# Weight loads moved to GpSimd's queue, three raw weight buffers for two, and v reordered from SyncE's queue

## The chip, the cores and the metric

The kernel runs on one core of one Trainium2 chip. The metric is the device time of one execution in microseconds (us). Before the change it is 1954.86 us, the median of three runs (1954.16 to 1957.37).

The engines are named TensorE (PE in the profile, PEld for its weight loads), VectorE (DVE), ScalarE (ACT), GpSimd (POOL) and SyncE (SP). SP computes nothing; it issues transfers, in the order of its program.

## The reference, cut to what matters

Two layers of a decoder trunk on 512 tokens of width 1024, in float32:

```python
for l in range(DEPTH):                                  # 2
    h = rms_norm(x, ln1_g[l])
    z = h @ w_in[l]
    xr, gr, q, k, v, g_rnn, g_att = jnp.split(z, cuts, axis=-1)
    xr = causal_depthwise_conv(xr, rnn_conv_w[l], rnn_conv_b[l])
    hr = rg_lru(xr, lru_wa[l], lru_ba[l], lru_wx[l], lru_bx[l], lru_lambda[l])
    y_rnn = hr * jax.nn.gelu(gr)
    y_att = dilated_attention_mixer(q, k, v, positions, q_norm_g[l], k_norm_g[l])
    merged = sigmoid(g_rnn) * (y_rnn @ proj_rnn[l]) + sigmoid(g_att) * (y_att @ proj_attn[l])
    x = x + merged @ w_out[l]
    h2 = rms_norm(x, ln2_g[l])
    u = causal_depthwise_conv(h2 @ w_up[l], ffn_conv_w[l], ffn_conv_b[l])
    u_gate, u_val = jnp.split(u, 2, axis=-1)
    x = x + (jax.nn.gelu(u_gate) * u_val) @ w_down[l]
```

The attention has three groups of four heads with dilations 1, 4 and 16; q and k are normalized and rotated. Groups with a dilation above 1 regroup the tokens into streams (t = m * dilation + r), so q, k and v have to be put into that order of tokens.

## The kernel before, in words

Every product of weights is made of three float32r matmuls: both operands are split into a high part and a low part, and high x high, high x low and low x high are summed. So a weight unit (256 rows x 512 columns, 512 KB) is loaded into a raw buffer `wraw`, ScalarE casts it to `whi` (line 229), VectorE subtracts to make `wlo` (line 234), and TensorE runs 24 matmuls with it (lines 259 to 261). There are some 320 units, in one fixed order, four (sometimes two or six) to a group of 512 output columns; `whi` and `wlo` have three buffers, `wraw` has RAW = 2.

In the loop over units, `prefetch_hi` casts the unit two ahead at the start of a unit, and `prefetch_lo`, in its middle, makes `wlo` of that unit and then calls `load(u + RAW)`. `load` (line 406) issues on SP. A buffer of `wraw` can be overwritten when `wlo` of the unit that lay in it is done, so SP's program holds a wait for VectorE ahead of each load.

A planner writes the order of the rest while the program is built. Work beside the matmuls is cut into chains; each step of a chain says which engine it needs, at what planned time (T["pe"], T["dve"], T["act"]) and how many buffers (20-odd `slot`s of 128x512, 12 `quad`s of 128x2048). Between matmuls `offer` takes the first chain whose step fits; a step for "pe" fits once TensorE's planned time is 1.5 us (MARGIN) past its due time. Engines then run their programs in order.

A step that the attention needs often is `turn` (line 376): VectorE transposes 32x32 blocks into a slot (line 382), SP issues four writes of 64 KB to HBM (line 388) and, one later step on, one read back (line 391); ScalarE copies the returned block (line 229) into a `quad`. There are 80 turns, 40 in each layer. SP also moves the statistics of the softmax (lines 781, 801, 802), the norm gains (line 613) and x.

v comes from groups v0, va and vb. `V.end` (line 705) marks a group done. For va and vb GpSimd's queue writes the four evicted blocks to HBM (line 711), waits until they have landed, and reads them back in the other order of tokens (line 712); `v_done[...].end` is the time at which the planner takes them for usable. `HOP` is 6500 ns.

Of the kernel before, what the change touches and what calls it, by code (L numbers as in the profile page):

```python
# [15 lines left out]
F32 = mybir.dt.float32  # L16
# [7 lines left out]
L, S, D, FF, NH = 2, 512, 1024, 3072, 12  # L24
EPS = 1e-6
BIG = 1e30
NQ = 12
NS = 21
LOOK = 2
RAW = 2  # L30
BACK = 1500.0
BACK_END = 600.0
MARGIN = 1500.0
HOP = 6500.0
# [23 lines left out]
IN_ORDER = ("N1", "N2", "v0")  # L58
# [118 lines left out]
def need(eng, t=0.0, at=0, s=0, q=0, y=0, after=()):  # L177

    return {"eng": eng, "t": t, "at": at, "s": s, "q": q, "y": y, "after": after}


def trunk(tc, wst, lruw, xT, pos, par, gqk, cst, yT):
    from contextlib import ExitStack
    nc = tc.nc
    with ExitStack() as ctx:
# [3 lines left out]
        dr = ctx.enter_context(tc.tile_pool(name="dr", bufs=4, space=bass.MemoryType.DRAM))  # L189
# [5 lines left out]
        for i in range(NQ):  # L195
            cp.tile([128, 4, 512], F32, name="quad", tag=f"quad{i}", bufs=1)
        for i in range(NS):
            cp.tile([128, 512], F32, name="slot", tag=f"slot{i}", bufs=1)
# [6 lines left out]
        T = {"pe": 0.0, "dve": 0.0, "act": 0.0, "table": ""}  # L205
# [22 lines left out]
        def copy(out, src, dep=0.0):  # L228
            nc.scalar.copy(out, src)  # L229
            T["act"] = max(T["act"], dep) + 93.0 + 0.834 * size(out)  # L230
            return T["act"]

        def tt(out, a, b, op, dep=0.0):
            nc.vector.tensor_tensor(out, a, b, op=op)  # L234
            return on_dve(size(out), dep)
# [19 lines left out]
        def rr(ap):  # L255
            return ap.bitcast(F32R)
# [29 lines left out]
        def start(gen, prio=None):  # L286
            if prio is None:
                serial[0] += 1
                prio = serial[0]
            c = Chain(gen, prio)  # L290
            c.step()
            if not c.done:
                chains.append(c)
                chains.sort(key=lambda c: c.prio)
            return c
# [48 lines left out]

        quads, sslots, place = list(range(NQ)), list(range(NS)), {}

# [52 lines left out]
        raws, halves, units = {}, {}, {}  # L399

        def load(upto):
            while unit_no[0] <= upto and unit_no[0] < NUNITS:
                u = unit_no[0]
                raws[u] = ring.tile([128, 1024], F32, name="wraw", tag="wraw", bufs=RAW)
                if u:
                    nc.sync.dma_start(raws[u], wst[u])
                else:
                    for k, queue in enumerate((nc.scalar, nc.sync)):
                        load_x(xT, nc.sync, k + 1)
                        queue.dma_start(raws[0][:, k * 512:k * 512 + 512], wst[0, :, k * 512:k * 512 + 512])  # L410
                unit_no[0] += 1

        def prefetch_hi(upto):
            while unit_no[1] <= upto and unit_no[1] < NUNITS:
                u = unit_no[1]
                load(u)
                raw = raws.pop(u)
                hi = whis[u % 3]
                halves[u] = (raw, hi, copy(rr(hi), raw, T["pe"] if u > LOOK else 0.0))
                unit_no[1] += 1  # L420

        def prefetch_lo():
            for u in list(halves):
                raw, hi, t = halves.pop(u)
                lo = wlos[u % 3]
                units[u] = (hi, lo, tt(rr(lo), raw, hi, ALU.subtract, t))
                load(u + RAW)

        x, xquad, at_x = [None] * 8, [], [0]

        def load_x(src, queue, upto=8):

            while len(xquad) < 2:
                q = qalloc()
                for i in range(4):
                    x[4 * len(xquad) + i] = q[:, i]
                xquad.append(q)
                at_x[0] = 0
            while at_x[0] < upto:
                c = at_x[0]  # L440
                queue.dma_start(x[c], src[c * 128:c * 128 + 128, :])
                at_x[0] += 1
# [14 lines left out]
        for i in range(9):  # L457
            nc.tensor.matmul(spin, idle[:, 0:128], idle, start=True, stop=True)
        nc.scalar.dma_start(prm[0][:, 0:P_CW], par[0, :, 0:P_CW])
        load(0)  # L460
        load(1)
        load_x(xT, nc.sync, 4)
# [141 lines left out]
        qkt, vt, yatt, rope_chain, att_chain, v_done = {}, {}, {}, {}, {}, {}  # L604

        class QK:
# [16 lines left out]
            def end(self):  # L623
                c = rope_chain[self.name] = start(self.chain())
                self.prio = c.prio
# [71 lines left out]
        class V:  # L697
# [6 lines left out]

            def end(self):
                vt[self.name] = self.t
                v_done[self.name].done = True
                v_done[self.name].end = T["act"]
                if self.name not in IN_ORDER:
                    d = dr.tile([S, 512], F32, name="vorder", tag="vorder", bufs=2)  # L710
                    nc.gpsimd.dma_start(d.rearrange("(b p) c -> p b c", p=128), self.t)
                    nc.gpsimd.dma_start(self.t, d.rearrange("(p r) c -> p r c", r=4))
                    v_done[self.name].end += 2 * HOP

        def score_steps(half, s, p0, st0):

# [444 lines left out]
        for k in range(2):  # L1161
            ks = slice(k * 512, k * 512 + 512)
            push(operand[k])
            t = copy(rr(hi[:, ks]), raw[:, ks])
            push(operand[k])
            t = tt(rr(lo[:, ks]), raw[:, ks], hi[:, ks], ALU.subtract, t)
# [13 lines left out]
        u = 0  # L1180
        for l, name, _, nk, k0, _ in GROUPS:
# [13 lines left out]
            for uu in range(nk // 2):  # L1195
# [38 lines left out]
                hi, lo, t = units.pop(u)  # L1234
# [62 lines left out]
```

## Time and profile before

| | us |
|---|---|
| median of three runs | 1954.86 |
| the profiled execution | 1954.35 |
| its span (first to last instruction) | 1952.6 |
| TensorE busy | 1868.8 |
| VectorE busy | 1306.6 |
| ScalarE busy | 967.2 |
| GpSimd busy | 5.6 |

The mean granted clock of TensorE is 0.978. The table is an average over stages that differ: the q, k, v projections with the attention (about 50 to 350 us, and 1020 to 1345 us in the second layer), the recurrent branch and the output projection, and the feed-forward part. The profile is read by stage, and an engine's idle time is followed back through the engine that it waited for, until a transfer or an engine that was busy ends the search.

### The profile page before, as it was taken

To read this page: it belongs to the slowest core of one execution; us is meant where nothing else is said; L and a number is where in the kernel's file an instruction comes from. 1 tells how busy PE (TensorE), PEld (TensorE's weight loads), DVE (VectorE), ACT (ScalarE), POOL (GpSimd) and SP (SyncE) were. 2 spreads that over 40 slices of the span, in tenths; PEclk is the share of its full clock that TensorE was granted. 3 is DMA by queue.
4 is the path that set the end of the run, shared out by engine and by line. 5 is a ranking of instruction groups with operands and counts; after the bars stand their busy time and mean duration, and the time that the engine had idled before them with its cause. 6 is when DMAs were issued, how large, how long until landed. Compare 5 with 4: busy or idle time off the path is not lost.

```text
span 1952.6 us, 22350 instructions
## 1 busy us (share of the span) xinstructions
PE 1868.8 (96%) x8249; PEld 1535.6 (79%) x8249; DVE 1306.6 (67%) x1938; ACT 967.2 (50%) x1655; POOL 5.6 (0%) x12
## 2 busy tenths in 40 slices
PE   9999888999899999999998998989989999999999
PEld 7777776887688888888887786778867888888887
DVE  7768886677656773577476697865875567635762
ACT  7567744577234442344364786455772444313431
POOL 0000000000000000000000000000000000000000
PEclk9999998999899999999999998989999999999999
DMA  4666655432322222222336566455223222322222
GB/s 170 161 172 171 174 137 133 128 111 83 111 95 97 98 97 97 98 97 95 121 121 167 169 162 172 135 137 152 83 76 120 96 98 98 107 98 87 97 104 91
DMA packets 244494, 235.01 MB, mean 120 GB/s; under 512 B 183456, under 2 KB 184736, under 8 KB 243872
## 3 DMA queue, kind: packets, MB, share of 16 engines
q1 hardware_dynamic: 238208, 224.89, 37.5%
q0 software_dynamic: 1664, 8.39, 1.2%
q8 instruction: 65, 1.06, 0.2%
q10 hardware_dynamic: 4512, 0.30, 0.2%
q14 instruction: 45, 0.37, 0.1%
HBM read 204.64 MB, written 28.88 MB: 120 GB/s over the span
## 4 chain that ended last, share of the span: by engine, by line
PE 69%; DVE 12%; DMA 8%; ACT 5%; SPq 4%; issue 2%; ACTq 0%; DVEq 0%
PE acc L259 22%; PE acc L260 22%; PE acc L261 22%; DVE slot L234 5%; DMA slot<-turn 3%; SPq L388 3%; DVE wlo L234 3%; DVE quad L234 2%; DMA turn<-slot 2%; ACT junk L223 1%; ACT whi L229 1%; ACT quad L229 1%; ACT quad L223 1%; DMA stats<-st 1%; DVE slot L382 1%
## 5 line engine op out<-in xcount | busy, mean ns | idle before, releaser
L229 ACT CAST whi<-wraw 128x1024 fp32r<-128x1024 f32 (+1 forms) x321 | 334.7, 1043 | 544.6 <-PE acc L260 482.6
L234 DVE TENSOR_TENSOR wlo<-wraw,whi 128x1024 fp32r<-128x1024 f32 (+1 forms) x321 | 390.0, 1215 | 206.7 <-ACT whi L229 206.6
L259 PE MATMUL acc<-xh,whi 128*128 128x512 f32 x1280 | 506.0, 395 | 13.7 <-ACT quad L223 10.8
L260 PE MATMUL acc<-xl,whi 128*128 128x512 f32 x1280 | 503.3, 393 | 0.0
L261 PE MATMUL acc<-xh,wlo 128*128 128x512 f32 x1280 | 503.1, 393 | 0.0
L259 PEld LDWEIGHTS acc<-xh,whi 128*128 128x128 f32 x1280 | 243.6, 190 | 65.8 <-ACT quad L223 12.9
L261 PEld LDWEIGHTS acc<-xh,wlo 128*128 128x128 f32 x1280 | 243.3, 190 | 51.6
L260 PEld LDWEIGHTS acc<-xl,whi 128*128 128x128 f32 x1280 | 243.6, 190 | 49.6
L259 PE MATMUL acc<-quad,whi 128*128 128x512 f32 x640 | 252.0, 394 | 22.1 <-ACT quad L229 22.0
L260 PE MATMUL acc<-quad,whi 128*128 128x512 f32 x640 | 251.8, 393 | 0.9 <-DVE quad L234 0.9
L261 PE MATMUL acc<-quad,wlo 128*128 128x512 f32 x640 | 250.6, 392 | 0.0
L259 PE MATMUL acc<-whi,xh 128*128 128x512 f32 x576 | 229.3, 398 | 11.6 <-ACT quad L223 6.0
L260 PE MATMUL acc<-wlo,xh 128*128 128x512 f32 x576 | 227.5, 395 | 4.8 <-DVE wlo L234 4.8
L261 PE MATMUL acc<-whi,xl 128*128 128x512 f32 x576 | 227.2, 394 | 0.0
L259 PEld LDWEIGHTS acc<-quad,whi 128*128 128x128 f32 x640 | 121.2, 189 | 51.0 <-ACT quad L229 26.1
L234 DVE TENSOR_TENSOR slot<-acc,rbc 128x512 f32<-128x512 f32 x112 | 77.1, 689 | 109.9 <-PE acc L261 109.9
L260 PEld LDWEIGHTS acc<-quad,whi 128*128 128x128 f32 x640 | 121.1, 189 | 28.9 <-DVE quad L234 3.9
L261 PEld LDWEIGHTS acc<-quad,wlo 128*128 128x128 f32 x640 | 121.2, 189 | 24.9
L259 PEld LDWEIGHTS acc<-whi,xh 128*128 128x128 f32 x576 | 109.8, 191 | 37.0 <-ACT quad L223 7.3
L260 PEld LDWEIGHTS acc<-wlo,xh 128*128 128x128 f32 x576 | 109.7, 190 | 28.5 <-DVE wlo L234 6.8
L229 ACT CAST quad<-slot 128x256 fp32r<-128x256 f32 (+1 forms) x104 | 62.3, 638 | 138.9 <-DMA slot<-turn 127.9
L261 PEld LDWEIGHTS acc<-whi,xl 128*128 128x128 f32 x576 | 109.5, 190 | 23.4
(136 smaller groups left out, 1940.9 us busy)
## 6 DMA issues: line engine op xcount, KB each, us to landing
wraw<-wst SPq DMA_DIRECT2D x319, 512.0 KB, 3.2
turn<-slot SPq DMA_DIRECT2D x288, 64.0 KB, 3.0
slot<-turn SPq DMA_DIRECT2D x48, 256.0 KB, 3.9
quad<-turn SPq DMA_DIRECT2D x24, 256.0 KB, 4.1
quad<-xT SPq DMA_DIRECT2D x16, 256.0 KB, 6.0
vorder<-quad POOLq DMA_DIRECT2D x4, 1024.0 KB, 7.1
quad<-vorder POOLq DMA_DIRECT2D x4, 1024.0 KB, 5.5
slot<-gqk SPq DMA_DIRECT2D x12, 256.0 KB, 3.6
```

The costliest lines, as they stand in the source:

```text
L223: nc.scalar.activation(out, src, func, **kw)
L229: nc.scalar.copy(out, src)
L234: nc.vector.tensor_tensor(out, a, b, op=op)
L259: nc.tensor.matmul(ps, rr(ah), rr(bh), start=first, stop=False)
L260: nc.tensor.matmul(ps, rr(ah), rr(bl), start=False, stop=False)
L261: nc.tensor.matmul(ps, rr(al), rr(bh), start=False, stop=last)
L382: nc.vector.transpose(w, t)
L388: nc.sync.dma_start(v[:, :, i], w[32 * i:32 * i + 32].rearrange("c (j e r) -> c j e r", j=n, e=4))
```

## The change

Four things in the diff. RAW becomes 3 and NS, the number of slots, 20. `load` issues unit 4 and later ones on GpSimd's queue, units 1 to 3 as before on SP. The reordering of va and vb becomes a chain of its own, `reorder`, with the highest priority: one step issues the write on SP once TensorE's planned time is 1.5 us past the planned eviction, another issues the read on SP 8 us of planned time later, and v counts as usable HOP after that. For v0 nothing is reordered, as before. The change's summary in words also names "a returning block expected one us later"; no line of the diff does that, and line 392 keeps its 4000.

```diff
-NS = 21
+NS = 20
 LOOK = 2
-RAW = 2
+RAW = 3
@@ load
                 if u:
-                    nc.sync.dma_start(raws[u], wst[u])
+                    (nc.sync if u < 4 else nc.gpsimd).dma_start(raws[u], wst[u])
                 else:
@@ class V
             def end(self):
                 vt[self.name] = self.t
+                if self.name not in IN_ORDER:
+                    start(self.reorder(T["act"]), 1)
+                else:
+                    v_done[self.name].done = True
+                    v_done[self.name].end = T["act"]
+
+            def reorder(self, t):
+                yield need("pe", t)
+                d = dr.tile([S, 512], F32, name="vorder", tag="vorder", bufs=2)
+                nc.sync.dma_start(d.rearrange("(b p) c -> p b c", p=128), self.t)
+                yield need("pe", T["pe"] + HOP)
+                nc.sync.dma_start(self.t, d.rearrange("(p r) c -> p r c", r=4))
                 v_done[self.name].done = True
-                v_done[self.name].end = T["act"]
-                if self.name not in IN_ORDER:
-                    d = dr.tile([S, 512], F32, name="vorder", tag="vorder", bufs=2)
-                    nc.gpsimd.dma_start(d.rearrange("(b p) c -> p b c", p=128), self.t)
-                    nc.gpsimd.dma_start(self.t, d.rearrange("(p r) c -> p r c", r=4))
-                    v_done[self.name].end += 2 * HOP
+                v_done[self.name].end = T["pe"] + HOP
```

## Rows read from the trace of the kernel before

**Rows 1.** Busy time by stretch (us); then TensorE's granted clock, DMA share, GB/s.

```profile
50.00:350.00 300.00, 271.35 (x1219) 222.75 (x1218) 229.10 (x408) 179.92 (x429) 2.75 (x4) 0.95 0.58 155
...
79.10:82.40 3.30, 3.30 (x10) 2.53 (x9) 1.80 (x4) 1.98 (x5) 0.00 (x0) 0.50 0.59 215
...
500.00:1020.00 520.00, 517.55 (x2281) 427.19 (x2280) 317.73 (x403) 204.58 (x270) 0.00 (x0) 1.00 0.30 104
1020.00:1345.00 325.00, 300.07 (x1338) 246.32 (x1337) 235.54 (x416) 196.18 (x445) 2.61 (x4) 0.95 0.58 158
```

**Rows 2.** Waits, whole span: waiter <- awaited: us in total, times, longest.

```profile
ACT quad L229 <- DMA slot<-turn: 127.9, 30, 10.0
```

**Rows 3.** SP's own waits, first in 50 to 350 us, then in 1020 to 1345.

```profile
SPq L406 <- DVE wlo L234: 64.8, 19, 8.6
...
SPq L406 <- DVE wlo L234: 82.9, 26, 10.1
```

**Rows 4.** Timeline, 52 to 80 us: start, us, engine, line; brackets: idle before, releaser.

```profile
55.13 1.89 DVE L382 STREAM_TRANSPOSE slot<-slot 128x512 f32<-128x512 f32 x3
...
52.02 9.35 SPq L406 DMA_DIRECT2D wraw<-wst  x2
61.41 8.18 SPq L388 DMA_DIRECT2D turn<-slot  x12
...
74.74 1.93 ACT L229 CAST quad<-slot 128x512 fp32r<-128x512 f32 x3 [7.89 <-DMA slot<-turn]
...
78.64 0.50 PE L259 MATMUL acc<-whi,xh 128*128 128x512 f32 x1 [3.42 <-ACT quad L223]
```

**Rows 5.** Timeline, 261 to 282 us.

```profile
261.05 0.71 DVE L382 STREAM_TRANSPOSE slot<-slot 128x512 f32<-128x512 f32 x1
...
266.38 0.33 SPq L406 DMA_DIRECT2D wraw<-wst  x1
266.76 3.11 SPq L388 DMA_DIRECT2D turn<-slot  x4
...
275.07 1.23 ACT L229 CAST quad<-slot 128x256 fp32r<-128x256 f32 x2 [9.51 <-DMA slot<-turn]
...
281.83 0.36 PE L754 MATMUL at<-quad 128*128 128x256 f32 x1 [2.96 <-DVE quad L234]
```

**Rows 6.** Timeline, 1195 to 1226 us.

```profile
1195.91 7.07 SPq L388 DMA_DIRECT2D turn<-slot  x10
...
1205.13 8.75 SPq L388 DMA_DIRECT2D turn<-slot  x12
...
1209.33 1.19 ACT L229 CAST quad<-slot 128x256 fp32r<-128x256 f32 x2 [4.83 <-DMA slot<-turn]
...
1222.23 1.19 ACT L229 CAST quad<-slot 128x256 fp32r<-128x256 f32 x2 [7.81 <-DMA slot<-turn]
...
1224.81 0.55 PE L851 MATMUL y<-quad 128*128 128x256 f32 x1 [4.55 <-DVE quad L234]
```

**Rows 7.** Issues and landings of writes (L388), loads (L406), v (L711, L712); ns min/median/max.

```profile
L388 SPq DMA_DIRECT2D turn<-slot x320: 569/627/2752, 61.4 to 1336.4; - x160
...
DMA to landing us min/median/max: 2.0/2.8/7.4
...
L406 SPq DMA_DIRECT2D wraw<-wst x319: 327/328/2384, 2.1 to 1923.5; - x160
...
wraw<-wst SPq DMA_DIRECT2D x319, 512.0 KB, 3.2
...
quad<-vorder POOLq DMA_DIRECT2D x4, 1024.0 KB, 5.5
...
L711 POOL DMA_DIRECT2D vorder<-quad x4: 757/757/891, 105.2 to 1213.8; - x4
L712 POOL DMA_DIRECT2D quad<-vorder x4: 547/548/549, 112.2 to 1222.5; - x4
...
DMA to landing us min/median/max: 5.0/6.6/8.2
```

## The prediction, made before the changed kernel was run

> **What bounds the kernel now.** I read the stretches first, then the waits, and last the timelines of SP's queue beside ScalarE and TensorE. From 500 to 1020 us TensorE is busy 517.55 of 520 us at full clock: 2281 matmuls, 0.227 us each, so a weight unit of 24 matmuls is 5.45 us, and nothing that only moves data makes this stretch shorter [rows 1]. The two attention stretches are different: 28.7 us idle of 300 and 24.9 us idle of 325, 53.6 us together, at a granted clock of 0.95. A mean of 0.95 between two levels of 1.0 and 0.5 is a tenth of the time at the lower one, 30 + 32.5 = 62.5 us, and one such short stretch is among the rows. At 90% busy, half speed loses 62.5 x 0.9 x 0.5 = 28 us. The attention stretches could thus give back at most 53.6 + 28 = 82 us. One long stall in each layer lies outside them, in the recurrent branch between ScalarE and VectorE; the change does not touch it.
>
> What makes TensorE idle there: ScalarE waits 127.9 us, 30 times, for a returned `slot<-turn` block [rows 2], and it is in order, so evictions and weight casts stand behind that wait. I followed the 19 idle times of TensorE over 0.8 us in the two stretches (50.7 us, first at 75, last at 1292) back the same way; 16 of them go to a late turn. Why late: SP issues the turn's four writes and its read, and also every weight load, and a load's line first waits until VectorE has finished `wlo` of the unit that held the buffer. In that one wait SP stands 64.8 of the 300 us and 82.9 of the 325 us [rows 3].
>
> Three cases. First: three transposes are done by 57.0 us, SP stands in line 406 from 52.0 to 61.4, the first write leaves at 61.4, ScalarE waits 7.89 us, TensorE 3.42 us [rows 4]. Second: transposed by 261.8, next a load that leaves at 266.4, writes at 266.8, ScalarE waits 9.51, TensorE 2.96 [rows 5]. Third, the other kind: between 1195.9 and 1213.9 SP issues 22 writes nearly back to back; a read behind them comes late, ScalarE waits 7.81, TensorE 4.55 [rows 6]. A write takes SP 0.63 us, a load 0.33 [rows 7].
>
> **The change part by part.** *Loads leave SP's queue.* From unit 4 on, line 406 issues on GpSimd's queue, which otherwise holds nothing any more. Behind a load's wait there now stand only later loads. For each of the 19 idle times I took from SP's timeline the time that SP spent in line 406 (waiting and issuing) between the transpose and its first write, and between the landing of the writes and the read; the saving is the smaller of this and the idle time. Example: rows 4 give 61.4 - 57.0 = 4.4 for the last of the three transposes and a microsecond more for the first, so all 3.42 go; rows 5 give 4.95, so all 2.96 go; rows 6 give only a load's issue on the write's way and one on the read's, 1.3 of 4.55. Summed so: 16.6 us in layer 0 and 13.1 us in layer 1, 29.7 of 50.7. Six of the 19 follow another within 14 us, and the turns behind them are already in flight when the earlier one is shortened; they carry 8.7 us, which I count at nothing. Left: 21 us. The lower clock comes behind such stalls (the stretch at 0.50 begins half a microsecond after the stall of 3.42 us ends, [rows 1, 4]), so I give back the same share, 28 x 21/53.6 = 11 us. What is late next is SP's own issue, four times 0.63 us for a turn, which stays.
>
> *Faster landing of turns.* Writes land in 2.0 us at best and 2.8 in the median [rows 7]. They no longer stand in one queue behind a 512 KB load, but the load still uses the same DMA engines. Bounds: 0.8 us for a write and as much for a read in each of the 19, 0 to 30 us, capped by the idle that is left; I take 0 and keep 15 for the range.
>
> *Does a load on GpSimd's queue come in time?* The trace has no load there. The nearest rows are the eight transfers of v, 1 MB each: issue 0.55 to 0.89 us, landing 5.0 to 8.2 us; the load itself lands from SP in 3.2 us in the median [rows 7]. So 3.5 to 9.1 us altogether; I take 4.5, nearer the row of the same size. With three raw buffers a load waits for the cast three units back, not two, and is needed 2.5 units later, not 1.5: 13.6 us against 8.2. Even 9.1 is covered: cost nothing, and the cover is gone above 13.6 us. ScalarE's waits for weights should nearly vanish, but they hardly ever end an idle time of TensorE, so I take nothing for them.
>
> *v goes through SP in two steps.* Two issues for each of four groups, about 0.76 + 0.55 us on SP [rows 7]. The write's step waits for ScalarE's last eviction of v, the read's step for the landing; behind either stand turns and the small transfers of the statistics. The write's wait: 0, or as long as ScalarE stood before such an eviction, 4.83 us [rows 6]; the code puts the step 1.5 us behind the planned eviction, so I take 1. The read's step comes 8 us after the write by the plan, and a landing takes up to 8.2 us [rows 7], so 0.2. Two of the four (the last, at 1213.8 us, and its twin in layer 0) fall into crowded stretches of SP: 2 x (1.31 + 1.2) = 5 us. Bounds 0 to 4 x (1.31 + 4.83) = 25 us. The users of v come a group later, so its planned end, some 3 us later, costs nothing.
>
> *20 slots for 21.* A gain is excluded, unless by a chance shift of order; a chain that finds no slot goes later. Bounds -5 to 10 us (one more wait as long as ScalarE's longest, [rows 2]); I take 0. *The first three loads* stay on SP, and the second of them no longer waits: 0, within 1 us either way.
>
> The sum: -21 - 11 + 5 = -27 us. The profiled execution took 1954.35 (span 1952.6 and 1.75 around it), 0.5 under the median of the three runs, so 1954.9 - 27 = 1928 us.
>
> **The rivals.** *All of it comes:* the six close stalls too (29.7, and 28 x 29.7/53.6 = 15 of clock), the landing 15, v free: 1954.9 - 60 = 1895. For it: SP's longest waits all go. Against: the third case. 0.13.
>
> *Little:* the load's line is only where SP happens to stand, and the turn waits as long elsewhere. Then only issue time is saved, two loads of 0.33 us in each of 13 stalls, 8.6 us, with 4 of clock, less 5 for v: 1947. For it: the third case, and 0.63 us for every write. Against: in one stretch SP waits 64.8 us in that line [rows 3], and its issues are 0.33. 0.12. The Trainium skill (DMA: Bandwidth & Descriptors, § Issuing engines are not separate DMA queues) says that issuing from several engines saves only the sequencer's issue time; by that rule this rival holds and the time is 1947. Rows 3 and 4 speak against the rule here, as what holds SP is a wait ahead of the issue.
>
> *Slower:* GpSimd's queue takes one load at a time. It decides from 5.45 us a load on, the time of a unit. If a load there took as long as v's read, 0.55 + 5.5 = 6.05 us [rows 7], then the 95 loads of 500 to 1020 us [rows 1] cost 0.6 us each, 57 us, and as much in the second layer: 1928 + 114 = 2042. For it: in the trace no two transfers of that queue are in flight together. Against: half the bytes, and 3.2 us from SP. 0.06. The Trainium skill (SBUF — State Buffer, § SBUF: two separate sides) says that VectorE can keep GpSimd from writing descriptors while an operation holds the port that they share; by that rule a load would come later by up to one operation of VectorE, and this rival would be likelier. Rows 7 show GpSimd's issues at 0.55 to 0.89 us in stretches where VectorE was busy three quarters of the time [rows 1], so no hold of that kind is seen.
>
> *The order shifts* with one slot less and v's later plan, and new stalls of the present size appear, eight of 3 us, 24, with 13 of their clock, beyond what is saved by 7: 1962. For it: the order is made by a greedy list. Against: nothing of the plan's engine times changes. 0.08. *The change doesn't do what it says:* its summary names a later return, which the diff lacks; I go by the diff, and no chance is kept for it.
>
> **How the numbers follow.** Forecast 1928 with 0.61, its own range 1911 to 1948 (landing 15, v's bound 20 more). All of it 0.13, little 0.12, slower 0.06 and 0.08. The range leaves out the first of the slower ones, half of the second, and part of the lower rival: 1900 to 1960. A measurement here can tell about 0.2% from no change, 3.9 us. Faster: 0.61 + 0.13 and a third of little, as 1947 with v at its bound is no gain, 0.78; same 0.07; slower 0.15.
>
> **What would show it.** Right: SP has no waits in line 406 in the attention stretches; the writes leave within 1 us of the transpose in the first two cases; ScalarE's wait for `slot<-turn` falls from 127.9 to about 80 us; TensorE's idle in the two stretches falls from 53.6 to about 37 us, the clock there rises from 0.95 to 0.97; the stretch from 500 to 1020 stays. Wrong: loads on GpSimd's queue land above 13 us, or ScalarE waits longer for weights; SP waits long in v's two steps; the writes leave late behind other lines.

## The result and the profile after

The changed kernel takes 1923.41 us, the median of four runs (1921.61 to 1927.58), beside 1956.11 us for the kernel before on the same chip (1954.16 to 1957.80). The ratio is 0.9836, 95% interval 0.9815 to 0.9857: 32 us faster, 28 to 36. The profiled execution of the changed kernel is the longest of its four, 1927.58 us with a span of 1925.6, against 1954.35 and 1952.6 before. Of all executions behind this document one, of the kernel raw3_late below, took 3107.92 us at a mean granted clock of 0.555, and is left out of its numbers.

First the sum. The page's line of busy times and the two shares of the chain that ended last, changed kernel:

```profile
PE 1859.5 (97%) x8249; PEld 1532.2 (80%) x8249; DVE 1306.7 (68%) x1938; ACT 969.2 (50%) x1655; POOL 167.9 (9%) x320
...
PE 79%; DVE 7%; ACT 5%; DMA 5%; SPq 2%; issue 2%; ACTq 0%; DVEq 0%
```

TensorE runs the same matmuls. Its busy time fell from 1868.8 to 1859.5 us (9.3), its idle time, span less busy, from 83.8 to 66.1 (17.7); together 27.0, the whole difference of the spans. So there is nothing to look for but two things: shorter stalls, and matmuls that run at a higher clock.

Second, where. Busy time by stretch, changed kernel; columns as in [rows 1]. The second attention stretch lies 20 us earlier here:

```profile
50.00:350.00 300.00, 281.08 (x1281) 232.81 (x1280) 238.26 (x424) 189.82 (x444) 23.86 (x45) 0.96 0.62 162
500.00:1000.00 500.00, 500.00 (x2209) 413.75 (x2208) 305.48 (x384) 197.24 (x256) 48.26 (x91) 1.00 0.29 101
1000.00:1325.00 325.00, 307.21 (x1411) 255.33 (x1410) 246.61 (x433) 204.54 (x460) 26.52 (x50) 0.97 0.62 164
```

The idle time of the two attention stretches is 18.9 + 17.8 = 36.7 us, where [rows 1] had 53.6; the clock is 0.96 and 0.97 for 0.95. The long stall of 9.01 us in the recurrent branch is still there, at 470.48 and 1425.08 us for 484.37 and 1453.01 before: 13.9 us were won ahead of it in the first layer and 14.0 more in the second; the parts behind the two stalls win nothing, as 27.0 of these 27.9 us are left at the end.

Third, the waits. Over the whole span, waiter, awaited, total, times, longest; then SP's own in 50 to 350 us:

```profile
ACT quad L229 <- DMA slot<-turn: 87.9, 28, 12.3
...
POOL wraw L406 <- DVE wlo L234: 1160.3, 231, 14.7
...
ACT whi L229 <- DMA wraw<-wst: 1.9, 2, 1.5
```

```profile
SPq L788 <- DMA stats<-st: 61.1, 4, 23.6
SPq L388 <- DVE slot L382: 55.5, 8, 44.1
SPq L391 <- DMA turn<-slot: 37.4, 29, 3.7
```

Line 406 is gone from SP's waits there [rows 3]; GpSimd now stands in that wait, for 1160.3 us, and only later loads stand behind it. ScalarE's wait for returned turns fell from 127.9 us [rows 2] to 87.9. SP's remaining waits belong to the turns and the statistics themselves. (Lines behind the diff are 7 higher: L788 was L781.)

Fourth, the three cases of [rows 4 to 6] again. Timelines of the changed kernel at 52 to 82 us, at 250 to 268 us and at 1182 to 1200 us:

```profile
55.51 1.89 DVE L382 STREAM_TRANSPOSE slot<-slot 128x512 f32<-128x512 f32 x3
56.25 8.17 SPq L388 DMA_DIRECT2D turn<-slot  x12
...
61.91 0.53 POOL L406 DMA_DIRECT2D wraw<-wst  x1 [8.71 <-ACT slot L223]
...
68.39 0.62 ACT L229 CAST quad<-slot 128x512 fp32r<-128x512 f32 x1 [1.18 <-DMA slot<-turn]
```

```profile
252.93 0.71 DVE L382 STREAM_TRANSPOSE slot<-slot 128x512 f32<-128x512 f32 x1
...
253.66 2.61 SPq L388 DMA_DIRECT2D turn<-slot  x4
...
260.54 1.23 ACT L229 CAST quad<-slot 128x256 fp32r<-128x256 f32 x2 [3.64 <-DMA slot<-turn]
```

```profile
1182.52 9.21 SPq L388 DMA_DIRECT2D turn<-slot  x12
1191.78 0.61 SPq L391 DMA_DIRECT2D slot<-turn  x1
...
1194.94 1.19 ACT L229 CAST quad<-slot 128x256 fp32r<-128x256 f32 x2 [4.66 <-DMA slot<-turn]
1197.52 0.36 PE L858 MATMUL y<-quad 128*128 128x256 f32 x1 [2.38 <-DVE quad L234]
```

In the first the writes leave while the second of the three transposes still runs, and the load that SP used to hold leaves from GpSimd at 61.91, after most of them. The copy shown waits 1.18 us, the longest in this window 3.11 (at 77.86), where one waited 7.89; and the largest idle time of TensorE up to 82 us is 0.90. In the second, transpose and write lie 0.02 us apart, ScalarE waits 3.64 us for 9.51, and TensorE does not stop. In the third the read leaves behind twelve writes that take SP 9.21 us, and 2.38 us remain of 4.55.

Not every stall became shorter. Two of TensorE's idle times grew by more than 2 us, at the same matmuls as before: from 0.87 to 4.60 us (103.18 us before) and from 4.19 to 6.62 (328.85 before). Changed kernel:

```profile
103.05 0.59 PE L259 MATMUL acc<-whi,xh 128*128 128x512 f32 x1 [4.60 <-ACT quad L223]
...
314.48 0.58 PE L858 MATMUL y<-quad 128*128 128x256 f32 x1 [6.62 <-ACT quad L229]
```

Last, issues and landings. From the two pages, median us from issue to landing, first before, then changed; and two lines' issue times in ns, changed:

```profile
turn<-slot SPq DMA_DIRECT2D x288, 64.0 KB, 3.0
slot<-turn SPq DMA_DIRECT2D x48, 256.0 KB, 3.9
```

```profile
wraw<-wst POOLq DMA_DIRECT2D x316, 512.0 KB, 3.5
turn<-slot SPq DMA_DIRECT2D x288, 64.0 KB, 3.7
slot<-turn SPq DMA_DIRECT2D x48, 256.0 KB, 3.5
```

```profile
L406 POOL DMA_DIRECT2D wraw<-wst x316: 530/530/664, 10.7 to 1891.6; - x158
...
L716 SPq DMA_DIRECT2D vorder<-quad x4: 374/408/1452, 104.8 to 1193.6; - x4
```

A load costs 0.53 us to issue from GpSimd and lands 3.5 us later, against 0.33 and 3.2 from SP [rows 7]. The writes of a turn now land later (3.7 for 3.0), the reads a little sooner (3.5 for 3.9).

### The profile page after: what moved, and what is told of

It reads as the page before. It is cut to its first block, busy times and chain, and to the rows that moved or that the text cites. A ratio compares the mean times of both kernels' runs of the same rounds, so it can differ in the third digit from the quotient of the medians.

```text
span 1925.6 us, 22502 instructions
## 1 busy us (share of the span) xinstructions
PE 1859.5 (97%) x8249; PEld 1532.2 (80%) x8249; DVE 1306.7 (68%) x1938; ACT 969.2 (50%) x1655; POOL 167.9 (9%) x320
## 4 chain that ended last, share of the span: by engine, by line
PE 79%; DVE 7%; ACT 5%; DMA 5%; SPq 2%; issue 2%; ACTq 0%; DVEq 0%
PE acc L259 26%; PE acc L260 25%; PE acc L261 25%; DVE slot L234 3%; SPq L388 2%; DMA slot<-turn 2%; ACT junk L223 2%; DVE wlo L234 1%; DVE quad L234 1%; DMA turn<-slot 1%; ACT whi L229 1%; ACT quad L229 1%; ACT quad L223 1%; ACT slot L229 1%; DVE quad L942 1%
## 5 line engine op out<-in xcount | busy, mean ns | idle before, releaser
L406 POOL DMA_DIRECT2D wraw<-wst x316 | 167.7, 531 | 1723.9 <-DVE wlo L234 1160.3
```

The source lines that it names most:

```text
L406: (nc.sync if u < 4 else nc.gpsimd).dma_start(raws[u], wst[u])
```

## The experiments

The theory on record (A): the gain comes from loads no longer standing, with their wait for VectorE, ahead of turns on SP. Its rivals: (B) it comes from the third raw buffer, that is from weights in time; (C) from v's new place; (H) from a second queue as such, since two queues are served side by side. (D) says that the weight traffic itself costs, whichever queue it is on. (In what was expected of reads_gp and writes_gp the letter C stands for H.)

All results in one table. A ratio is to the kernel before, run beside each on the same chip, where its median was 1953.79 to 1956.11. TensorE's idle time is span less busy time of the profiled run. The mean turn is my working from the timelines: for each of the 80 turns, from the end of its transpose to the landing of its read, averaged.

| kernel | median us | ratio to before, 95% | TensorE idle | ScalarE's wait for turns | mean turn |
|---|---|---|---|---|---|
| before | 1954.86 | | 83.8 | 127.9 | 15.99 |
| raw3_sp | 1954.43 | 1.0004 (0.9993 to 1.0016) | 86.0 | 127.8 | 16.06 |
| v_sp | 1951.80 | 0.9985 (0.9973 to 0.9998) | 82.9 | 114.9 | 16.02 |
| loads_gp_raw2 | 1923.50 | 0.9836 (0.9807 to 0.9866) | 65.8 | 73.4 | 14.48 |
| v_gp | 1930.48 | 0.9876 (0.9849 to 0.9904) | 73.4 | 96.1 | 14.63 |
| the change | 1923.41 | 0.9836 (0.9815 to 0.9857) | 66.1 | 87.9 | 14.44 |
| raw3_late | 1918.66 | 0.9808 (0.9788 to 0.9828) | 59.3 | 85.3 | 14.09 |
| writes_gp | 1935.69 | 0.9901 (0.9884 to 0.9918) | 68.4 | 104.6 | 13.78 |
| reads_gp | 1921.91 | 0.9840 (0.9824 to 0.9857) | 60.7 | 96.7 | 14.09 |
| half_loads | 1894.13 | 0.9698 (0.9683 to 0.9712) | 45.0 | 59.9 | 12.80 |
| double_loads | 1994.15 | 1.0195 (1.0174 to 1.0217) | 113.2 | 134.3 | 17.95 |
| ret5 | 1912.57 | 0.9787 (0.9772 to 0.9801) | 61.6 | 85.9 | 14.08 |
| swap | 1914.24 | 0.9794 (0.9779 to 0.9810) | 58.8 | 84.0 | 13.52 |
| swap_ret5 | 1902.88 | 0.9737 (0.9717 to 0.9757) | 51.0 | 73.3 | 13.49 |

### Which part of the change carries the gain

**raw3_sp**: the kernel before with three raw buffers and 20 slots; loads stay on SP, v on GpSimd.

```diff
-NS = 21
+NS = 20
-RAW = 2
+RAW = 3
```

> The kernel before with three raw buffers and 20 slots; loads stay on SP, v on GpSimd's queue. Theory A: no gain, 1950 to 1960 us, since load(u + RAW) still stands on SP behind the wlo that has just been put out, so SP's wait in line 406 stays near 65 and 83 us in the two attention stretches, while ScalarE's wait for weights (20.6 us) falls to about 5 us. Rival B: about 1925 us.

Measured: 1954.43, ratio 1.0004. The profile says why. Waits over the whole span, and SP's in 50 to 350 us:

```profile
ACT quad L229 <- DMA slot<-turn: 127.8, 30, 10.0
...
ACT whi L229 <- DMA wraw<-wst: 2.1, 2, 1.3
```

```profile
SPq L406 <- DVE wlo L234: 65.6, 16, 8.6
```

The third buffer does what it is for: ScalarE's waits for weights go from 20.6 us in 12 times to 2.1 in 2. The time does not move. And SP stands in line 406 as long as before: `load` is called right behind the `wlo` that frees its buffer, with three buffers as with two. B falls, and the slot taken away costs nothing that shows.

**loads_gp_raw2**: the change with the old two buffers and 21 slots.

```diff
-NS = 20
+NS = 21
-RAW = 3
+RAW = 2
```

> The change with two raw buffers and 21 slots, as in the kernel before: only the queue of the loads and v's two steps are changed. Theory A (SP no longer stands ahead of turns in a load's wait): nearly all of the gain stays, 1922 to 1932 us; a load then has 8.2 us instead of 13.6 us between release and use and takes about 4 us, so ScalarE's wait for weights stays under 20 us. Rival B (the third buffer, by earlier loads, is what gains): 1945 us or more.

Measured: 1923.50, ratio 0.9836, the same as the change, though ScalarE's waits for weights are back (22.3 us, 14 times). Loads and v together, without the buffer, give all of it.

**v_sp**: the kernel before with v's reordering on SP alone. Its edit is shown against the change.

```diff
-NS = 20
+NS = 21
-RAW = 3
+RAW = 2
@@ load
-                    (nc.sync if u < 4 else nc.gpsimd).dma_start(raws[u], wst[u])
+                    nc.sync.dma_start(raws[u], wst[u])
```

> The kernel before with only v's reordering moved to SP in two steps. By the prediction's term: 5 us slower than before, 1960 us (bounds 1955 to 1980). If the transfers of v on GpSimd's queue had disturbed the turns: faster than 1951 us.

Measured: 1951.80, ratio 0.9985, an interval that just leaves out 1: 2 to 3 us faster, by the interval 0.4 to 5. The prediction's five lost microseconds are not there.

**v_gp**: the change with v's two transfers back on GpSimd's queue, among the loads. Its edit is shown against the kernel before.

```diff
-NS = 21
+NS = 20
-RAW = 2
+RAW = 3
@@ load
-                    nc.sync.dma_start(raws[u], wst[u])
+                    (nc.sync if u < 4 else nc.gpsimd).dma_start(raws[u], wst[u])
```

> The changed kernel with v's reordering back on GpSimd's queue, where loads now stand behind v's wait of some 7 us for its own landing, four times. By the prediction's term of 5 us for v on SP, and loads covered by 13.6 us: 1915 to 1921 us. If the loads held back there count: 1925 us or more, and ScalarE's wait for weights above 20 us.

Measured: 1930.48, 7 us over the change; the ranges of the runs (1927.21 to 1933.57, 1921.61 to 1927.58) overlap at one end, as do those of v_gp and loads_gp_raw2 (1920.88 to 1929.20), so the size of this difference is uncertain. TensorE's idle time is 7.3 us more. ScalarE's waits for weights stay at 1.9 us, so it is not that loads stand behind v's wait and come late; the longest landing of a load is 10.0 us, well inside their cover. ScalarE's wait for turns is longer, 96.1 us for 87.9, but that sum alone does not give the time: loads_gp_raw2 has 73.4 and reads_gp 96.7 beside the time of the change. Where the 7 us come from was not found.

So the loads alone are worth 1954.9 x (1 - 0.9876) = 24 us (19 to 30 by the interval), v on SP beside them some 7, and buffer and slot nothing.

### The wait or the queue

In the change the load's wait leaves SP and the load gets a queue of its own. raw3_late takes away only the wait: the loads stay on SP, three buffers, and each load is called one unit later than three buffers would allow, so that the `wlo` it waits for was finished about a unit before.

**raw3_late**:

```diff
-NS = 21
+NS = 20
-RAW = 2
+RAW = 3
@@ prefetch_lo
-                load(u + RAW)
+                load(u + RAW - 1)
```

> The kernel before with three raw buffers and 20 slots, and the load called one unit later (load(u + RAW - 1)): it then waits for a wlo that is a unit old, so the wait is over when SP comes to it. Queue, bytes and the load's deadline (1.5 units) stay as in the kernel before; all loads stay on SP. It separates the wait from the queue. Theory A (what costs is the wait ahead of a load): SP's wait for wlo in line 406 below 15 us in each attention stretch (64.8 and 82.9 before), a turn's time from transpose to first write down by about 1 us, and most of the gain without a second queue: 1930 to 1942 us. Rival H (a second queue is what gains, because transfers of one queue stand in line): 1948 to 1958 us.

Measured: 1918.66, ratio 0.9808, at or a little below the change and below the 1930 to 1942 expected, with everything on SP that was there before. Timeline from 50 to 66 us, and SP's wait in line 406 in 50 to 350 us:

```profile
53.23 0.33 SPq L406 DMA_DIRECT2D wraw<-wst  x1
...
56.35 1.89 DVE L382 STREAM_TRANSPOSE slot<-slot 128x512 f32<-128x512 f32 x3
57.08 8.08 SPq L388 DMA_DIRECT2D turn<-slot  x12
```

```profile
SPq L406 <- DVE wlo L234: 25.4, 10, 7.9
```

The first case is healed as in the change: the load leaves at 53.23, ahead of the transposes, and the writes at 57.08. My number for the waits was wrong, 25.4 us where under 15 were expected, but these are not the waits that count: the time that line 406 holds SP waiting between a transpose and its first write, summed over all turns, fell from 83.1 us to 3.7. H falls, as far as this gain goes: no second queue is needed for it. Against raw3_sp, one term in one call is worth 36 us. In the mean of the 80 turns the first write leaves 2.02 us sooner (3.10 us behind the transpose for 5.12), half of which is the wait itself, and the landings are much as they were (writes 2.81 us for 2.85, reads 4.17 for 4.06). So the gain lies ahead of the first write and not in faster transfers. The page's line for the writes, to hold beside the 3.0 and 3.7 above:

```profile
turn<-slot SPq DMA_DIRECT2D x288, 64.0 KB, 2.7
```

**writes_gp** is the mirror: the change, with the turns' writes on GpSimd's queue, behind the loads and their wait; reads stay on SP.

```diff
@@ turn
-                nc.sync.dma_start(v[:, :, i], w[32 * i:32 * i + 32].rearrange("c (j e r) -> c j e r", j=n, e=4))
+                nc.gpsimd.dma_start(v[:, :, i], w[32 * i:32 * i + 32].rearrange("c (j e r) -> c j e r", j=n, e=4))
```

> The changed kernel with the turns' writes (line 388) on GpSimd's queue beside the loads; the reads stay on SP. It corrects the mirror test: in the kernel before, a load's line held a turn 1.4 us ahead of its first write and only 0.4 us ahead of its read, so only the writes should suffer. Theory A: the mean from transpose to first write, 3.5 us in the changed kernel and 5.0 in the one before, comes back to 5 us or more, a turn takes 16 us again and not 14.4, and the time is 1940 to 1960 us. Rival C (spreading issues over two queues is what gains): 1912 to 1926 us.

Measured: 1935.69, 12 us over the change, less than the 17 to 37 expected. The first two cases are back, on another engine. Timelines from 50 to 66 us and from 253 to 272 us:

```profile
55.19 1.89 DVE L382 STREAM_TRANSPOSE slot<-slot 128x512 f32<-128x512 f32 x3
...
61.57 0.53 POOL L406 DMA_DIRECT2D wraw<-wst  x1 [8.70 <-ACT slot L223]
62.10 4.44 POOL L388 DMA_DIRECT2D turn<-slot  x6
```

```profile
255.49 0.71 DVE L382 STREAM_TRANSPOSE slot<-slot 128x512 f32<-128x512 f32 x1
...
261.48 0.55 POOL L406 DMA_DIRECT2D wraw<-wst  x1 [6.74 <-issue]
262.02 2.98 POOL L388 DMA_DIRECT2D turn<-slot  x4
```

The transposes are done, and the writes leave half a microsecond behind a load that stood still 8.70 and 6.74 us. From transpose to first write the mean is 4.87 us, as before the change (5.02; 3.52 in the change); line 406 holds GpSimd for 2.32 of them, by the same working as the 83.1 us above, its issues counted in. But with SP free of writes a read goes out 0.20 us after the writes have landed, not 1.42, and the mean turn is shorter than in the change, 13.78. The time is longer all the same: a mean over 80 turns does not say which of them somebody waits for. ScalarE's wait for turns is 104.6 us, 16.7 over the change, but as reads_gp shows (96.7 us and no slower), that sum does not order the kernels either.

**reads_gp**: the change, with the turns' reads on GpSimd's queue.

```diff
@@ turn
-            nc.sync.dma_start(t, d)
+            nc.gpsimd.dma_start(t, d)
```

> The changed kernel with the turns' reads (line 391) issued on GpSimd's queue, where they stand behind the loads' waits as they stood on SP before; the same bytes, the same planned order. Theory A (what costs is to stand behind a load's wait): slower than the changed kernel's 1923.5 by 10 to 40 us, 1935 to 1965 us, and ScalarE's wait for returned blocks back above 110 us. Rival C (the gain came from spreading issues over two queues, whatever stands in them): not slower, 1915 to 1926 us, since SP has 80 issues less.

Measured: 1921.91, no slower; a miss. In the kernel before, line 406 stood ahead of a read 0.36 us per turn (12.9 us of waiting and 15.7 of issuing over 80), ahead of a first write 1.43 us: there the damage was in the writes. In reads_gp itself the reads do meet loads, 0.81 us per turn, yet they leave no later behind the landing of the writes than in the change (1.43 us in the mean for 1.42), and SP, without them, issues the first write 2.43 us behind the transpose for 3.52. So this run does not show what a load's wait ahead of a read alone would cost.

### What the traffic itself costs

**half_loads**: the change, every second load left out from unit 7.

```diff
@@ load
+                if u >= 6 and u % 2:
+                    raws[u] = raws[u - 1]
+                    unit_no[0] += 1
+                    continue
```

> The changed kernel with every second weight load left out from unit 7 on (the unit before it is used twice, so the output is another one). All matmuls, casts and turns stay. It halves the weight traffic beside the turns, whose writes land in 3.7 us in the median now and landed in 3.0 before. Theory D (the turns' landing beside the loads is part of what is still lost): writes land in under 3.2 us and the time is 5 to 12 us below the changed kernel, 1911 to 1919 us. Rival E (SP's own issue of the writes is all that is left): within 3 us of the changed kernel, 1920 to 1927 us.

Measured: 1894.13, 29 us under the change; no theory had that. **double_loads** goes the other way: every unit is loaded a second time into a buffer that nobody reads (two raw buffers, which cost nothing in loads_gp_raw2).

```diff
-RAW = 3
+RAW = 2
@@ load
+                    if u >= 6:
+                        nc.gpsimd.dma_start(ring.tile([128, 1024], F32, name="extra", tag="extra", bufs=1), wst[u])
```

> The changed kernel with two raw buffers (alone no different from it, 1923.5 us) and, from unit 6 on, every weight unit loaded a second time into a buffer that nobody reads. Over the kernels so far a turn's mean time from transpose to landed read and the time go together: 16.0 us and 1954, 14.4 and 1923, 12.8 and 1894, some 19 us for each us of a turn. Theory D (weight traffic lengthens a turn's landings, and through them the time): the turn at 15.5 to 17 us and 1945 to 1970 us, all of it in the attention stretches, while 500 to 1000 us stays at full rate. Rival G (leaving out loads helped in another way, by GpSimd's or VectorE's waits): within 5 us of 1923.

Measured: 1994.15, 71 us over the change, beyond the expected 1945 to 1970. Busy time by stretch, half_loads and then double_loads (an attention stretch, the feed-forward stretch, the other attention):

```profile
50.00:330.00 280.00, 271.82 (x1264) 225.94 (x1263) 233.67 (x420) 187.02 (x441) 11.66 (x22) 0.98 0.52 128
500.00:980.00 480.00, 480.00 (x2120) 397.31 (x2120) 289.84 (x362) 187.15 (x234) 23.33 (x44) 1.00 0.16 54
980.00:1300.00 320.00, 313.33 (x1465) 261.06 (x1464) 254.50 (x446) 211.77 (x478) 13.79 (x26) 0.99 0.51 127
```

```profile
50.00:350.00 300.00, 260.04 (x1140) 211.85 (x1140) 216.49 (x380) 172.68 (x410) 43.10 (x82) 0.93 0.79 225
500.00:1000.00 500.00, 488.03 (x2128) 401.23 (x2127) 302.66 (x379) 188.26 (x220) 92.57 (x176) 0.99 0.56 193
1060.00:1380.00 320.00, 281.00 (x1252) 230.09 (x1251) 219.90 (x390) 184.55 (x412) 47.32 (x90) 0.94 0.77 221
```

In the feed-forward stretch the traffic goes from 54 to 193 GB/s and TensorE does not mind (of double_loads' missing 12 us there, 9.01 are the recurrent stall, which lies inside that window, and 1.95 the idle time next to it). Nearly all of it comes from the attention, where the idle time goes from 8.2 + 6.7 = 14.9 us to 40.0 + 39.0 = 79.0; over the whole span it goes from 45.0 to 113.2. Late weights are hardly the reason: ScalarE waits for them 25.6 us, 13 times, in double_loads, and 22.3 us, 14 times, in loads_gp_raw2. The landings say how. The page's lines for writes and reads of turns, half_loads first:

```profile
turn<-slot SPq DMA_DIRECT2D x288, 64.0 KB, 2.6
slot<-turn SPq DMA_DIRECT2D x48, 256.0 KB, 3.0
```

```profile
turn<-slot SPq DMA_DIRECT2D x288, 64.0 KB, 5.0
slot<-turn SPq DMA_DIRECT2D x48, 256.0 KB, 4.2
```

A write lands in 2.6, 3.7 and 5.0 us with half, all and twice the weight traffic, a read in 3.0, 3.5 and 4.2, and the median time follows: 1894, 1923, 1994. The loads are on another queue in all three. D holds, and larger than I had it; with the loads on SP's queue it was not tried. The Trainium skill (DMA: Bandwidth & Descriptors, § Issuing engines are not separate DMA queues) says that transfers issued by different engines run on the same 16 DMA engines and interleave there; the three landings agree. Where on the way they meet, the runs don't tell.

### What is left to take

**swap**: the roles changed over. SP issues loads alone; turns and v go through GpSimd's queue.

```diff
@@ turn
-                nc.sync.dma_start(v[:, :, i], w[32 * i:32 * i + 32].rearrange("c (j e r) -> c j e r", j=n, e=4))
+                nc.gpsimd.dma_start(v[:, :, i], w[32 * i:32 * i + 32].rearrange("c (j e r) -> c j e r", j=n, e=4))
-            nc.sync.dma_start(t, d)
+            nc.gpsimd.dma_start(t, d)
@@ load
-                    (nc.sync if u < 4 else nc.gpsimd).dma_start(raws[u], wst[u])
+                    nc.sync.dma_start(raws[u], wst[u])
@@ reorder
-                nc.sync.dma_start(d.rearrange("(b p) c -> p b c", p=128), self.t)
+                nc.gpsimd.dma_start(d.rearrange("(b p) c -> p b c", p=128), self.t)
...
-                nc.sync.dma_start(self.t, d.rearrange("(p r) c -> p r c", r=4))
+                nc.gpsimd.dma_start(self.t, d.rearrange("(p r) c -> p r c", r=4))
```

> All weight loads stay on SP as before; the turns' writes and reads and v's two steps go to GpSimd's queue instead, with 3 raw buffers and 20 slots. Theory A: separation is what counts and not which queue the loads are on, so about the gain of the change, 1920 to 1935 us, if GpSimd issues a write of 512 pieces in about the 0.76 us of v's write and not much above SP's 0.63. If a GpSimd write costs 1 us or more, SP's place as the next limit moves there and the time is 1940 us or more.

Measured: 1914.24, ratio 0.9794, faster than the change and than the 1920 to 1935 expected. A write's issue is dearer, and its landing sooner than in the change. Line 388 in ns, and the page's landings:

```profile
L388 POOL DMA_DIRECT2D turn<-slot x320: 678/742/885, 56.2 to 1291.6; - x160
```

```profile
turn<-slot POOLq DMA_DIRECT2D x288, 64.0 KB, 3.2
slot<-turn POOLq DMA_DIRECT2D x48, 256.0 KB, 3.3
```

**ret5**: the change with what its summary names and its diff lacks, the return expected one us later, so that the planner puts ScalarE's copy later.

```diff
@@ turn
-            return T["pe"] + 4000.0
+            return T["pe"] + 5000.0
```

> The changed kernel with the planner expecting a returned block 1 us later (5000 for 4000 in line 392), the step that the change's summary names and the diff lacks. A turn still takes 14.4 us in the mean from transpose to landing, and ScalarE still waits 87.9 us for 28 blocks, 3.1 us each. Theory A': each wait shrinks by up to 1 us, up to 28 us of ScalarE's waits, of which perhaps a third reaches TensorE: 1912 to 1922 us. Rival: the order of the list changes by chance: 1915 to 1935 us either way.

Measured: 1912.57, ratio 0.9787, 11 us under the change. How it comes is not shown: ScalarE's wait for turns hardly falls (85.9 us in 21 times for 87.9 in 28), while TensorE's idle time is 4.5 us shorter and its busy time 10.0 (1849.5 for 1859.5). Later copies or a luckier order of the list, no run tells them apart.

**swap_ret5** does both: to the edit of swap it adds

```diff
@@ turn
-            return T["pe"] + 4000.0
+            return T["pe"] + 5000.0
```

> The exchange of queues (loads on SP, turns and v on GpSimd; 1914.2 us) with a returned block expected 1 us later (which took 10.9 us from the changed kernel). If the two add: 1902 to 1908 us. If both take the same waits of ScalarE: 1909 to 1915 us.

Measured: 1902.88, ratio 0.9737 (0.9717 to 0.9757). The two gains add, and it is the fastest kernel of the study that computes everything: 52 us under the kernel before, 20 under the change. ScalarE's wait for turns is 73.3 us in 20 times, TensorE's idle time 51.0 us.

## Why the prediction was right

The forecast was 1928 us in 1900 to 1960, faster by 27 us; the profiled execution is faster by 26.8, the medians by 32. The mechanism was right; that the sum fits so closely is in part luck, as two terms are off in opposite ways. By its steps:

**The main step holds, and its place.** SP stood in a load's wait while finished transposes stood behind it. Three runs carry this: raw3_late takes the wait from ahead of the writes, with queue and bytes as before, and gains 36 us, writes_gp puts it ahead of the writes on another engine and loses 12, raw3_sp gives weights more time without moving the wait and gains nothing. All signs that were named for it came: no wait of SP in line 406, writes within a microsecond of the transposes, idle time 53.6 to 36.7 (37 foretold), clock 0.96 and 0.97 (0.97), a full stretch from 500 us on. ScalarE's wait fell to 87.9, not quite to 80.

**The two large terms, -21 and -11,** can be read directly: idle time down 17.7, busy time of the same matmuls down 9.3. But these include what v did, and there two errors cancel. Stall by stall, at the same matmuls, the fit is also less close than in sum: of the 19 idle times the 13 that were counted go from 34.9 to 18.5 us, 16.4 saved where 21 was forecast, with the two that grew among them; the six close ones, counted at nothing, go from 15.8 to 10.8 (two are gone, 1.10 and the second case's 2.96, one is halved, three stay or grow); and four new ones over 0.8 us add 5.7.

**v on SP was mis-sized, with the wrong sign.** The term was +5, from issue time and a wait as long as the plan's 1.5 us miss ScalarE. Measured: -2 to -3 alone, and 7 us lost when it goes back to GpSimd beside the loads. The larger figure rests on overlapping runs. The bound "0 to 25" should have reached below nothing: the change also moves v's wait and the time at which its users are planned, and I excluded a gain without a row. The cost side is seen to be small: the two issues take 0.41 and 0.46 us in the median, and the slowest write step 1.45; SP waits 1.2 us, once, ahead of the write's step.

**So the loads were mis-sized too:** 24 us (v_gp) where -21 and -11 gave 32. Part of it is in the landing, which I had taken at 0 with a gain as the only bound. By the mean turn the change wins 1.50 us ahead of the first write and 0.46 ahead of the read, and pays 0.21 between first and last write and 0.22 in the landings (writes 0.66 later, reads 0.44 sooner). And raw3_late, with v where v_gp has it and no second queue for the loads, won 36: its first writes leave 0.37 us sooner than v_gp's and its writes land 0.86 us sooner, its reads 0.50 later. So 32 is no bad size for the wait itself, and the second queue seems to cost some 12 us that the prediction held at nothing; which of these differences carries them is not shown.

**The zero terms:** a load on GpSimd takes 0.53 + 3.5 = 4.0 us where 4.5 was taken, and nobody waits for it (1.9 us in 2 times). The slot and the third buffer cost and give nothing (loads_gp_raw2, raw3_sp).

**The rivals.** *Little*, 1947, is out: what holds a queue is the wait ahead of the issue and not the issue. The rule of the Trainium skill (DMA: Bandwidth & Descriptors, § Issuing engines are not separate DMA queues), that issuing from several engines only saves issue time, gave 1947 here; the loads' move alone reached 1930 (v_gp), so the rule misses what stands ahead of an issue. That the saving does not need a second engine, raw3_late shows. *One load at a time* is out, by 4.0 us a load against 5.45. The Trainium skill (SBUF — State Buffer, § SBUF: two separate sides) says that VectorE can keep GpSimd from writing descriptors while it runs operations of one kind. Line 406 takes 530 ns at least and in the median and 664 at most, and lands in 3.3 us at best and 3.5 in the median, with VectorE busy 238.26 of 300 us in the first attention stretch, so most loads show no such hold; whether VectorE ran operations of that kind, no run shows. *All of it*, 1895, is what swap_ret5 and half_loads come near, by other means. *The order shifts* did not make the kernel slower, though single stalls grew. Its sum was wrong: 24 and 13, less the 27 saved, is 10, which makes 1965 and not 1962; and the forecast's own range, 15 below 1928, begins at 1913 and not 1911. Nothing hung on either.

**Left open:** why v on GpSimd's queue beside the loads costs some 7 us; why writes land later when the loads are on GpSimd (3.7) than when both are on SP (3.0, and 2.7 in raw3_late) or changed over (3.2); and which turns make writes_gp slower than its mean turn.

## What to carry to other kernels

When an engine's program issues transfers for two purposes, look at what stands ahead of each issue: a wait for an engine, put there by the one that has time, holds the one that has none, and the cure is to issue the patient transfer where its wait is already over, by one buffer more and a call one step later; another queue frees it too, but is not what counts, and here it took 12 us less off the time (v_gp and raw3_late). In a stage bound by the latency of small round trips, price the large transfers beside them by the landing of the small ones, for here half the weight traffic was worth nearly as much as the whole change (29 us and 32). And undo each part by itself even when the sum comes out right: here +5 was -2 to -7, and 32 was 24.

## What the runs showed of the hardware

- Weight traffic on another queue lengthens small transfers below full use of the DMA engines: at a DMA share of 0.52, 0.62 and 0.79 in the first attention stretch, a 64 KB write of a turn landed in 2.6, 3.7 and 5.0 us, the median over both layers.
- The same write costs SP 0.63 us to issue and GpSimd 0.74, and the 512 KB load 0.33 and 0.53; yet the kernel with the turns on GpSimd's queue and the loads on SP's is the faster one, 1914 us against 1923.
- A third of the change's gain in the profiled run is clock: the same 8249 matmuls took 9.3 us less, with the granted clock in the attention up from 0.95 to 0.96 and 0.97 as the stalls became fewer. It is one pair of profiles: raw3_sp, which is no faster than the kernel before, shows 1866.2 us where that has 1868.8.
